# Block sums of the modulation vectors on VectorE in the feed-forward, and later sums with four rows a recurrence step in the first mixer

## The chip, the cores and the metric

The kernel runs on one core of one Trainium2 chip. The metric is the device time of one execution in microseconds (us). The engines are TensorE (PE, whose weight loads are shown apart as PEld), VectorE (DVE), ScalarE (ACT), GpSimd (POOL) and SyncE (SP), whose queue issues most of the DMAs.

## What is computed

The reference is a trunk of two decoder layers over 256 tokens of width 2048, in fp32. Cut to what matters here:

```
cond = silu(c)
for l in range(2):
    mod = (cond @ w_ada[l] + b_ada[l]).reshape(6, 2048)
    sh_m, sc_m, gt_m, sh_f, sc_f, gt_f = mod
    u = x * (1 + sc_m) + sh_m
    proj = u @ w_in[l]
    y_attn = sliding_window_attention(proj ...)      # 16 heads
    y_rwkv = rwkv7_group(proj ...)                   # 16 heads, a recurrence over the tokens
    x = layer_norm(a * x + gt_m * (concat(y_attn, y_rwkv) @ w_out[l]))
    u = x * (1 + sc_f) + sh_f
    x = layer_norm(a * x + gt_f * ((silu(u @ w_gate) * (u @ w_up)) @ w_down[l]))
```

The change concerns the first line of the loop alone: a vector of 2048 numbers times a matrix of 2048 x 12288, for each layer. That matrix is 96 MB a layer and is read once; its product is small, but each of the six pieces is needed at its own point of the layer, so the kernel spreads the work over the run.

## The kernel before

**The weight stream.** All big products go through one scheme. A raw fp32 weight tile comes in by DMA (128 x 1024, four buffers), ACT rounds it to a high part (line 435, three buffers), DVE subtracts to get the low part (line 436, two buffers), and PE makes three matmuls for each piece (lines 457, 458, 460: high by high, high by low, low by high). One such step in the feed-forward is twelve matmuls of 512 columns. PE is to run from step to step without a hole.

**The modulation vectors.** They are made beside that stream in units: a unit is one of the six pieces of one layer, half of it, 1024 columns. For a unit, a generator (`ada_steps`, lines 255 to 281) takes sixteen row steps. Each row step loads 128 rows of the unit (one DMA of 512 KB into the tile `ast`) and makes one DVE operation that adds row times its number of `cond`, per partition, onto the accumulator `aacc` (128 x 1024; line 268 for the first row, line 270 for the rest). Then come `LAG` = 2 empty steps, and then the sum over the 128 partitions. `ada_sums` (lines 316 to 341) does it thus: PE transposes the eight blocks of 128 x 128 (line 327, two PSUM banks of four), ACT copies each with an accumulating output, which adds up its columns (line 331), DVE adds the bias into `mods` (line 334). For a gate (pieces 2 and 5) PE transposes the result (line 339) and a DMA puts it aside as a row.

Two units of the first layer ((0,3,0) and (0,4,1): layer, piece, half) take another way, `ada_direct`: four PE matmuls a row onto four quarters of a bank (`gv`, line 290), with `cond` as the weights.

**What drives the row steps.** In the weight stream `pump` advances the generator by a pace a step (0.75 in the feed-forward of layer 0). In the recurrence of the mixers it is advanced by `adv(AR[l])` at each of the four steps of a recurrence, and in attention by `adv(AA[l])`. The units run in a fixed list, `ada_rest`: in the first mixer (0,2,0), (0,2,1), (0,4,0), then the two direct ones and (0,3,1), then eleven from (0,5,0) on beside the feed-forward of layer 0, and three in the second mixer. `done` holds the finished units; four are finished before the first mixer begins. `side` is set while a feed-forward runs (line 1266, cleared at 1342); then the row tiles take turns between two pools.

**What sets the order.** Within a mixer a string, `ORDER[l]`, gives the order of its operations, which is the order in which the code emits instructions. The final order on each engine is that of a scheduler which simulates when each instruction could run. So an instruction that is emitted elsewhere, or costs something else, can move others.

**Around it.** In the recurrence (lines 837 to 889) PE makes `mr` (lines 841 and 848) for a pair of heads, and then for each of four steps `ob` (lines 868, 871) and the new state `db` (lines 878, 882), which ACT copies. Line 775 is another small product of the same stage, and line 963 a set of transposes for attention. Before the feed-forward and before the next mixer, the residual and the layer norm run on DVE (lines 1335 to 1338, 1132 to 1146), and PE transposes the normalised rows (line 409). There, and only there, the kernel issues matmuls with no use but to keep PE busy: `warm` (lines 104 to 107), eleven before the feed-forward of layer 0 and eight before the second mixer. They write a PSUM bank of the ring from which the sums take theirs.

Of the kernel before, what the change touches and what calls it, by code (L numbers as in the profile page):

```python
# [10 lines left out]
F32 = mybir.dt.float32  # L11
# [3 lines left out]
ALU = mybir.AluOpType  # L15
# [4 lines left out]
P = 128  # L20
# [25 lines left out]
LAG = 2  # L46
WB = (4, 3, 2)
RED = 1
AR = (3, 7)
AA = (1, 45)  # L50
AP = (0.65, 0.3)
AO = (1.1, 2.9)
# [17 lines left out]
def hybrid_trunk_kernel(  # L70
# [21 lines left out]
    def bank(name="mb", tag="mb"):  # L92

        if tag == "cb":
            return ps.tile([P, 512], F32, tag="cb", name=name)
        t = f"m{turn[0]}"
        turn[0] ^= turn[1]
        return ps.tile([P, 512], F32, tag=t, name=name, bufs=1)
# [64 lines left out]
    def prm(l, nm, i, n=1):  # L163
        o = PC[nm] + i
        return par[l][:, o // P, o % P:o % P + n]
# [90 lines left out]
    def ada_steps(l, mod, c0):  # L256

        src = w_ada[l].rearrange("(j p) n -> p j n", p=P)
        n0 = mod * D + c0
        if direct[0]:  # L260
            yield from ada_direct(l, mod, c0, src[:, :, n0:n0 + 1024])
            return
        acc = adap.tile([P, 1024], F32, tag="aacc", name="aacc")
        for j in range(KT):
            t = (side[j % 2:] or [adap])[0].tile([P, 1024], F32, tag="ast", name="ast", bufs=2)
            fetch(t, src[:, j, n0:n0 + 1024], j < 2 and not done)
            if j == 0:
                V.tensor_scalar_mul(acc, t, cond[:, 0:1])
            else:
                ins = V.scalar_tensor_tensor(acc, t, cond[:, j:j + 1], acc, ALU.mult, ALU.add)  # L270
                if anchor:
                    tc.add_manual_dep(ins.ins, anchor[0], order, reason="behind the weight stream")
            yield
        for _ in range(LAG):
            yield

        ada_sums(l, mod, c0, [acc[:, i * P:(i + 1) * P] for i in range(8)])
        done.add((l, mod, c0 // 1024))
        yield

    def ada_direct(l, mod, c0, src):
# [31 lines left out]
        done.add((l, mod, c0 // 1024))  # L313
        yield

    def ada_sums(l, mod, c0, blocks, idle=0):

        col = mod * KT + c0 // P
# [15 lines left out]
        V.scalar_tensor_tensor(mods[l][:, col:col + n], sm[:, 0:n], 1.0 if mod in (1, 4) else 0.0,  # L334
                               prm(l, "b_ada", col, n), ALU.add, ALU.add)
        if mod in (2, 5):
            row = adap.tile([8, P], F32, tag="arow", name="arow", bufs=2)[0:n]
            rb = bank()
            PE.transpose(rb[0:n, 0:P], mods[l][:, col:col + n], ident)
            S.copy(row, rb[0:n, 0:P])  # L340
            dma(gates[l, mod // 3, c0 // P:c0 // P + n], row)

    lead = []

# [1082 lines left out]
```

## Time and profile before

| | |
|---|---|
| median of three runs | 2636.09 us (2634.07 to 2643.67) |
| the profiled execution | 2648.1 us, its span 2646.4 us, mean granted PE clock 0.975 |
| PE busy | 2504.7 us, 95% of the span |
| DVE busy | 1805.9 us, 68% |
| ACT busy | 1185.7 us, 45% |

The profile is that of one execution. A line of it names the engine, the line of the code, the operation, output<-input, and "xN" for N records; an fp32 matmul that is no transpose shows as two records. "[6.26 <-DVE aacc L270]" says that the engine stood idle 6.26 us before this instruction, until DVE had finished the tile aacc on line 270. The granted clock is a share of the full rate.

### The profile page before, as it was taken

To read this page: it belongs to the slowest core of one execution; us is meant where nothing else is said; L and a number is where in the kernel's file an instruction comes from. 1 tells how busy PE (TensorE), PEld (TensorE's weight loads), DVE (VectorE), ACT (ScalarE), POOL (GpSimd) and SP (SyncE) were. 2 spreads that over 40 slices of the span, in tenths; PEclk is the share of its full clock that TensorE was granted. 3 is DMA by queue.
4 is the path that set the end of the run, shared out by engine and by line. 5 is a ranking of instruction groups with operands and counts; after the bars stand their busy time and mean duration, and the time that the engine had idled before them with its cause. 6 is when DMAs were issued, how large, how long until landed. Compare 5 with 4: busy or idle time off the path is not lost.

```text
span 2646.4 us, 42219 instructions
## 1 busy us (share of the span) xinstructions
PE 2504.7 (95%) x15619; PEld 2084.7 (79%) x15619; DVE 1805.9 (68%) x2439; ACT 1185.7 (45%) x2023; POOL 144.7 (5%) x368
## 2 busy tenths in 40 slices
PE   3798998999999999999999999989899999999997
PEld 3797785677888888888888887867788888888887
DVE  7977766579877777777787776565855455545456
ACT  2464453435544444444444544544444443344442
POOL 1003222000000000000000023120000000000000
PEclk9898998999999999999999999989999999999999
DMA  9987657698998888888878685425656655566554
GB/s 371 343 256 238 192 184 248 213 342 289 360 336 304 305 305 312 307 293 308 300 242 301 198 274 163 126 55 202 217 192 189 193 186 194 193 191 191 190 188 147
DMA packets 336384, 637.50 MB, mean 241 GB/s; under 512 B 59511, under 2 KB 126515, under 8 KB 334643
## 3 DMA queue, kind: packets, MB, share of 16 engines
q1 hardware_dynamic: 333170, 629.05, 70.9%
q0 software_dynamic: 1280, 2.62, 0.4%
q10 hardware_dynamic: 1728, 3.15, 0.3%
q8 instruction: 122, 2.00, 0.3%
q14 instruction: 84, 0.68, 0.1%
HBM read 622.08 MB, written 12.62 MB: 240 GB/s over the span
## 4 chain that ended last, share of the span: by engine, by line
PE 79%; DMA 10%; DVE 5%; issue 2%; POOL 2%; ACT 1%; SPq 0%; DVEq 0%; POOLq 0%; ACTq 0%
PE acc L458 20%; PE acc L457 20%; PE acc L460 20%; DMA ast<-in_w_ada_dram 5%; PE acc L471 3%; PE acc L470 3%; PE acc L469 3%; DVE lo L436 1%; DMA raw<-in_w_out_dram 1%; POOL tmp L790 1%; POOL ttl L792 1%; PE mb L1296 1%; DVE aacc L270 1%; PE gv L290 1%; DVE aacc L358 1%
## 5 line engine op out<-in xcount | busy, mean ns | idle before, releaser
L436 DVE TENSOR_TENSOR lo<-raw,hi 128x1024 fp32r<-128x1024 f32 (+2 forms) x728 | 882.0, 1212 | 561.3 <-PE acc L458 375.6
L435 ACT CAST hi<-raw 128x1024 fp32r<-128x1024 f32 (+2 forms) x728 | 758.1, 1044 | 1042.7 <-PE acc L460 836.3
L458 PE MATMUL acc<-lo,u 128*128 128x512 f32 x1568 | 512.8, 394 | 7.8 <-DVE lo L436 7.8
L460 PE MATMUL acc<-hi,u 128*128 128x512 f32 x1568 | 505.7, 391 | 0.0
L457 PE MATMUL acc<-hi,u 128*128 128x512 f32 x1568 | 458.8, 394 | 2.0 <-ACT sg L1289 1.2
L270 DVE SCALAR_TENSOR_TENSOR aacc<-ast,cond,aacc 128x1024 f32<-128x1024 f32 x270 | 345.3, 1279 | 38.9 <-DMA ast<-in_w_ada_dram 38.2
L458 PEld LDWEIGHTS acc<-lo,u 128*128 128x128 f32 x1568 | 294.4, 189 | 71.0 <-DVE lo L436 10.4
L457 PEld LDWEIGHTS acc<-hi,u 128*128 128x128 f32 x1568 | 295.2, 189 | 64.9 <-ACT sg L1289 1.6
L460 PEld LDWEIGHTS acc<-hi,u 128*128 128x128 f32 x1568 | 295.2, 188 | 61.5 <-issue 0.2
L458 PE MATMUL acc<-lo,ht 128*128 128x512 f32 (+1 forms) x720 | 243.3, 377 | 1.5 <-DVE lo L436 1.5
L460 PE MATMUL acc<-hi,ht 128*128 128x512 f32 (+1 forms) x720 | 242.2, 375 | 0.0
L457 PE MATMUL acc<-hi,ht 128*128 128x512 f32 (+1 forms) x720 | 217.0, 376 | 0.0
L469 PE MATMUL acc<-u,hi 128*128 128x256 f32 x720 | 202.9, 289 | 1.9 <-ACT hi L435 1.8
L470 PE MATMUL acc<-u,hi 128*128 128x256 f32 x720 | 202.2, 288 | 0.0
L471 PE MATMUL acc<-u,lo 128*128 128x256 f32 x720 | 190.6, 291 | 5.2 <-DVE lo L436 5.0
L458 PEld LDWEIGHTS acc<-lo,ht 128*128 128x128 f32 x720 | 135.1, 188 | 26.9 <-DVE lo L436 3.1
L460 PEld LDWEIGHTS acc<-hi,ht 128*128 128x128 f32 x720 | 135.6, 188 | 24.3
L457 PEld LDWEIGHTS acc<-hi,ht 128*128 128x128 f32 x720 | 134.8, 188 | 24.3
L469 PEld LDWEIGHTS acc<-u,hi 128*128 128x128 f32 x720 | 141.0, 196 | 5.9 <-ACT hi L435 2.5
L470 PEld LDWEIGHTS acc<-u,hi 128*128 128x128 f32 x720 | 141.0, 196 | 2.8 <-issue 1.7
L471 PEld LDWEIGHTS acc<-u,lo 128*128 128x128 f32 x720 | 132.3, 196 | 9.8 <-DVE lo L436 6.7
L1135 POOL TENSOR_TENSOR brs<-brs,mhalf 128x1 f32<-128x1 f32 x8 | 6.3, 786 | 1685.9 <-DVE brs L1134 765.1
(358 smaller groups left out, 2916.3 us busy)
## 6 DMA issues: line engine op xcount, KB each, us to landing
ast<-in_w_ada_dram SPq DMA_DIRECT2D x368, 512.0 KB
raw<-in_w_gate_up_dram SPq DMA_DIRECT2D x704, 256.0 KB
raw<-in_w_down_dram SPq DMA_DIRECT2D x176, 512.0 KB
raw<-in_w_in_dram SPq DMA_DIRECT2D x82, 512.0 KB
raw<-in_w_out_dram SPq DMA_DIRECT2D x64, 512.0 KB
raw<-in_w_in_dram SPq DMA_DIRECT2D x120, 256.0 KB
ast<-in_w_ada_dram SPq DMA_DIRECT2D x32, 256.0 KB
lnw<-in_ln_w_dram SPq DMA_DIRECT2D x4, 1024.0 KB
```

The source lines that it names most:

```text
L270: ins = V.scalar_tensor_tensor(acc, t, cond[:, j:j + 1], acc, ALU.mult, ALU.add)
L290: PE.matmul(gv[32 * q:32 * q + 32, 0:T], lhsT=cond[:, j:j + 1].to_broadcast([P, 32]), rhs=t[:, q * T:(q + 1) * T], start=(j == 0), stop=(j ...
L358: V.scalar_tensor_tensor(acc, t[:, j], cond[:, j0 + j:j0 + j + 1], acc, ALU.mult, ALU.add)
L435: S.copy(h, fl)
L436: ins = V.tensor_tensor(r, fl, h.bitcast(F32), ALU.subtract)
L457: PE.matmul(bt, lhsT=xh, rhs=hi[:, c0:c0 + w], start=st, stop=False)
L458: PE.matmul(bt, lhsT=xh, rhs=lo[:, c0:c0 + w], start=False, stop=False)
L460: PE.matmul(banks[t][q][:, 0:w], lhsT=xl, rhs=hi[:, c0:c0 + w], start=False, stop=sp_)
L469: PE.matmul(bt, lhsT=hi[:, c0:c0 + w], rhs=xh, start=st and opens, stop=False)
L470: PE.matmul(bt, lhsT=hi[:, c0:c0 + w], rhs=xl, start=False, stop=False)
L471: PE.matmul(bt, lhsT=lo[:, c0:c0 + w], rhs=xh, start=False, stop=sp_ and closes)
L790: G.tensor_tensor(tmp[:, 0:cm, 0:w], nb[:, s:s + 1, s + 1:].to_broadcast([P, cm, w]), tt[:, 0:cm, s:s + 1].to_broadcast([P, cm, w]), ALU.mult)
```

## The change

There are three edits.

1. `AR` goes from (3, 7) to (4, 7): at each recurrence step of the first mixer four rows are asked for, where it was three.
2. The empty steps between the last row of a unit and its sums are six (`3 * LAG`), where they were two, for the units that are reached with at most eight units done and outside a feed-forward: (0,2,0), (0,2,1) and (0,4,0). Inside a feed-forward and later they stay two.
3. Inside a feed-forward the sums over the partitions are made by a new function, `block_sums`. DVE transposes each 32 x 32 block of a half of the accumulator (128 x 512) in one operation, so that the 32 partitions of a block lie along the free axis, and reduces them to 16 numbers; so each of the four groups of 32 partitions has its own partial sum. Four PE matmuls with `fold`, four identity matrices of 32 x 32 stacked over the partitions, add the four groups and put each quarter of the columns on its own 32 output partitions. `fold` is made anew for each unit by three small DVE additions.

```diff
@@ -46,7 +46,7 @@
 LAG = 2
 WB = (4, 3, 2)
 RED = 1
-AR = (3, 7)
+AR = (4, 7)
 AA = (1, 45)
 AP = (0.65, 0.3)
 AO = (1.1, 2.9)
@@ -271,10 +271,13 @@
                 if anchor:
                     tc.add_manual_dep(ins.ins, anchor[0], order, reason="behind the weight stream")
             yield
-        for _ in range(LAG):
+        for _ in range(LAG if side or len(done) > 8 else 3 * LAG):
             yield
 
-        ada_sums(l, mod, c0, [acc[:, i * P:(i + 1) * P] for i in range(8)])
+        if side:
+            block_sums(l, mod, c0, acc, side[1])
+        else:
+            ada_sums(l, mod, c0, [acc[:, i * P:(i + 1) * P] for i in range(8)])
         done.add((l, mod, c0 // 1024))
         yield
 
@@ -313,6 +316,34 @@
         done.add((l, mod, c0 // 1024))
         yield
 
+    def block_sums(l, mod, c0, acc, fp):
+
+        col = mod * KT + c0 // P
+        fold = fp.tile([P, 32], F32, tag="fold", name="fold", bufs=1)
+        V.tensor_add(fold, ident[:, 0:32], ident[:, 32:64])
+        for g in (64, 96):
+            V.tensor_add(fold, fold, ident[:, g:g + 32])
+        part = fp.tile([P, 32], F32, tag="apart", name="apart", bufs=1)
+        for q in range(2):
+            tr = fp.tile([P, 512], F32, tag="atr", name="atr", bufs=1)
+            V.transpose(tr, acc[:, q * 512:(q + 1) * 512])
+            V.reduce_sum(part[:, q * 16:(q + 1) * 16], tr.rearrange("p (b r) -> p b r", r=32), axis=AX.X)
+        b = bank()
+        for q in range(4):
+            PE.matmul(b[32 * q:32 * q + 32, 0:8], lhsT=fold, rhs=part[:, q::4], start=True, stop=True)
+        V.scalar_tensor_tensor(mods[l][:, col:col + 8], b[:, 0:8], 1.0 if mod in (1, 4) else 0.0, prm(l, "b_ada", col, 8), ALU.add, ALU.add)
+        if mod in (2, 5):
+            gate_sums(l, mod, c0, 8)
+
+    def gate_sums(l, mod, c0, n):
+
+        col = mod * KT + c0 // P
+        row = adap.tile([8, P], F32, tag="arow", name="arow", bufs=2)[0:n]
+        rb = bank()
+        PE.transpose(rb[0:n, 0:P], mods[l][:, col:col + n], ident)
+        S.copy(row, rb[0:n, 0:P])
+        dma(gates[l, mod // 3, c0 // P:c0 // P + n], row)
+
     def ada_sums(l, mod, c0, blocks, idle=0):
 
         col = mod * KT + c0 // P
@@ -334,11 +365,7 @@
         V.scalar_tensor_tensor(mods[l][:, col:col + n], sm[:, 0:n], 1.0 if mod in (1, 4) else 0.0,
                                prm(l, "b_ada", col, n), ALU.add, ALU.add)
         if mod in (2, 5):
-            row = adap.tile([8, P], F32, tag="arow", name="arow", bufs=2)[0:n]
-            rb = bank()
-            PE.transpose(rb[0:n, 0:P], mods[l][:, col:col + n], ident)
-            S.copy(row, rb[0:n, 0:P])
-            dma(gates[l, mod // 3, c0 // P:c0 // P + n], row)
+            gate_sums(l, mod, c0, n)
 
     lead = []
 
```

After line 315 the lines of the new kernel have other numbers: 327 is now 358, 409 is 436, 436 is 463, 457, 458 and 460 are 484, 485 and 487; in the recurrence 841, 848, 868, 871, 878, 882 and 290 are 868, 875, 895, 898, 905, 909 and 293.

**In the recurrence of the first mixer.** On PE, the place where the sums of (0,4,0) stand (`mb<-ident,aacc`), between the parts of `mr` of the third group of heads and its first recurrence steps; `gv` are the row sums of the next, direct unit. Before:

```order
L848 MATMUL mr<-am,ah 64x64 x2
L327 MATMUL mb<-ident,aacc 128x128 x4
L848 MATMUL mr<-am,ah 64x64 x3
L775 MATMUL bnb<-xr,bones 128x256
L848 MATMUL mr<-am,ah 64x64
L841 MATMUL mr<-bkt,ah 128x128 x2
L848 MATMUL mr<-am,ah 64x64 x6
L290 MATMUL gv<-ast,cond 32x256 x6
L327 MATMUL mb<-ident,aacc 128x128 x4
L290 MATMUL gv<-ast,cond 32x256 x2
L871 MATMUL ob<-uv,am 64x64 x4
L878 MATMUL db<-uv,bkt 64x64 x4
```

After:

```order
L875 MATMUL mr<-am,ah 64x64 x6
L358 MATMUL mb<-ident,aacc 128x128 x3
L802 MATMUL bnb<-xr,bones 128x256
L358 MATMUL mb<-ident,aacc 128x128
L868 MATMUL mr<-bkt,ah 128x128 x2
L875 MATMUL mr<-am,ah 64x64 x6
L898 MATMUL ob<-uv,am 64x64 x4
L358 MATMUL mb<-ident,aacc 128x128 x4
L905 MATMUL db<-uv,bkt 64x64 x4
L293 MATMUL gv<-ast,cond 32x256 x8
L895 MATMUL ob<-state_1664,rh 64x128 x2
L898 MATMUL ob<-uv,am 64x64 x4
```

The first transposes move from behind two of the `mr` matmuls to behind six, the second four from ahead of `ob` to behind it, and the row sums `gv` from ahead of `ob` and `db` to behind them.

The rest of that recurrence on PE: `state` is the state that ACT copied from the step before. Before:

```order
L963 MATMUL acc<-ident,qr 128x128 x6
L868 MATMUL ob<-state_1664,rh 64x128 x2
L871 MATMUL ob<-uv,am 64x64 x4
L878 MATMUL db<-uv,bkt 64x64 x2
L882 MATMUL db<-state_1664,mt 64x64 x2
L878 MATMUL db<-uv,bkt 64x64 x2
L882 MATMUL db<-state_1664,mt 64x64 x2
L868 MATMUL ob<-state_1665,rh 64x128 x2
L871 MATMUL ob<-uv,am 64x64 x4
```

After:

```order
L905 MATMUL db<-uv,bkt 64x64 x2
L909 MATMUL db<-state_1664,mt 64x64 x2
L293 MATMUL gv<-ast,cond 32x256 x4
L895 MATMUL ob<-state_1665,rh 64x128 x2
L898 MATMUL ob<-uv,am 64x64 x4
L905 MATMUL db<-uv,bkt 64x64 x2
L909 MATMUL db<-state_1665,mt 64x64 x2
L905 MATMUL db<-uv,bkt 64x64 x2
L909 MATMUL db<-state_1665,mt 64x64 x2
L293 MATMUL gv<-ast,cond 32x256 x4
L895 MATMUL ob<-state_1664,rh 64x128 x2
```

Between the recurrence steps stand `gv` rows, one at each step, where before none stood there until the recurrence was over.

**In the feed-forward.** On DVE, the end of one unit and the beginning of the next, in the feed-forward of layer 0: `lo<-raw,hi` is the low part of a weight tile. Before:

```order
L436 TENSOR_TENSOR lo<-raw,hi 128x1024
L270 SCALAR_TENSOR_TENSOR aacc<-ast,cond,aacc 128x1024
L436 TENSOR_TENSOR lo<-raw,hi 128x1024 x3
L268 TENSOR_SCALAR aacc<-ast,cond 128x1024
L334 SCALAR_TENSOR_TENSOR mods_128<-asum,par_124 128x8
L436 TENSOR_TENSOR lo<-raw,hi 128x1024
```

After:

```order
L463 TENSOR_TENSOR lo<-raw,hi 128x1024
L270 SCALAR_TENSOR_TENSOR aacc<-ast,cond,aacc 128x1024
L329 STREAM_TRANSPOSE atr<-aacc 128x512
L463 TENSOR_TENSOR lo<-raw,hi 128x1024
L330 TENSOR_REDUCE apart<-atr 128x16
L329 STREAM_TRANSPOSE atr<-aacc 128x512
L463 TENSOR_TENSOR lo<-raw,hi 128x1024
L330 TENSOR_REDUCE apart<-atr 128x16
L268 TENSOR_SCALAR aacc<-ast,cond 128x1024
L463 TENSOR_TENSOR lo<-raw,hi 128x1024 x2
L334 SCALAR_TENSOR_TENSOR mods_128<-mb,par_124 128x8
```

The two block transposes and the two reductions stand between the low parts of three weight tiles. On PE the four matmuls of this unit (`mb<-apart,fold`) stand ahead of the first matmul that reads the low part made next after line 268; so it is in ten of the eleven units, or with a longer distance, and in the last they stand among the last matmuls of `w_down`.

**Keep-warm matmuls of the second mixer.** On PE, `mb<-rmask,ident`, before the transposes of the normalised rows (`mb<-ident,z`). Before:

```order
L458 MATMUL acc<-wl,ht 128x256
L460 MATMUL acc<-wl,ht 128x256
L107 MATMUL mb<-rmask,ident 128x256 x8
L409 MATMUL mb<-ident,z 128x128 x8
L469 MATMUL lb<-u,hi 128x256
```

After, the same place, and then one of the two places in the stream of `w_down` to which four each have gone:

```order
L484 MATMUL acc<-wl,ht 128x256
L485 MATMUL acc<-wl,ht 128x256
L487 MATMUL acc<-wl,ht 128x256
L436 MATMUL mb<-ident,z 128x128 x8
L496 MATMUL lb<-u,hi 128x256
```

```order
L487 MATMUL acc<-hi,ht 128x512 x2
L484 MATMUL acc<-hi,ht 128x512 x4
L107 MATMUL mb<-rmask,ident 128x256 x4
L485 MATMUL acc<-lo,ht 128x512 x2
L487 MATMUL acc<-hi,ht 128x512 x2
L485 MATMUL acc<-lo,ht 128x512 x2
```

All eight have moved up, some 450 matmuls ahead. Of the eleven before the feed-forward of layer 0, two have moved up among the last matmuls of the output projection in the same way, and nine stand where they stood.

## Prediction

> **What bounds the kernel now.** First the page: engine totals and the chain that ended last.
>
> ```profile
> span 2646.4 us, 42219 instructions
> PE 2504.7 (95%) x15619; PEld 2084.7 (79%) x15619; DVE 1805.9 (68%) x2439; ACT 1185.7 (45%) x2023; POOL 144.7 (5%) x368
> PE 79%; DMA 10%; DVE 5%; issue 2%; POOL 2%; ACT 1%; SPq 0%; DVEq 0%; POOLq 0%; ACTq 0%
> ```
>
> TensorE (PE) is busy 95% of the span. An average hides the stages, so next the windows (columns: length, then busy time of PE, PEld, DVE, ACT and POOL, granted PE clock, DMA share, GB/s).
>
> ```profile
> 400.00:500.00 100.00, 87.63 (x993) 57.50 (x992) 65.19 (x199) 40.79 (x141) 15.94 (x38) 0.88 0.74 233
> 700.00:800.00 100.00, 100.00 (x459) 82.74 (x458) 72.68 (x69) 46.78 (x76) 0.00 (x0) 1.00 0.89 320
> ```
>
> From 700 us on, the feed-forward of layer 0, PE has no hole at full clock (the windows up to 1300 read alike): a microsecond of PE work taken out there is a microsecond of the run, one put in costs as much, and DVE has about 27% of idle time. The recurrence, 400 to 500, is a stage of waits at a reduced clock. PE's waits there and in the output projection behind it:
>
> ```profile
> PE mb L327 <- DVE aacc L270: 6.3, 1, 6.3
> PE acc L457 <- ACT hi L435: 4.3, 2, 4.0
> PE mb L409 <- DVE z L1146: 2.5, 2, 1.7
> PE gv L290 <- DMA ast<-in_w_ada_dram: 2.3, 3, 1.2
> PE ob L868 <- ACT state L887: 2.0, 3, 1.1
> ```
>
> Those five are what the second half of the change could win.
>
> **a. Sums in the feed-forward.** Eleven units lose eight 128x128 transposes on PE and get four 32x8 matmuls. The timeline of PE around one unit before:
>
> ```profile
> 723.43 0.60 PE L327 MATMUL mb<-ident,aacc 128*128 128x128 f32 x4
> ...
> 729.85 1.07 PE L457 MATMUL acc<-hi,u 128*128 128x512 f32 x4
> 732.57 1.07 PE L457 MATMUL acc<-hi,u 128*128 128x512 f32 x4
> ```
>
> A weight step of twelve matmuls is 732.57 - 729.85 = 2.72 us. From 723.43 to 729.85 lie two steps and the eight transposes (four in this row, four in one like it that is left out): 6.42 - 5.44 = 0.98 us a unit. The trace has no 32x8 matmul. Its nearest rows, each plain fp32 matmul being two records:
>
> ```profile
> 179.21 0.63 PE L701 MATMUL ssb<-bones,kkn 128*64 128x2 f32 x8
> 179.76 0.38 PE L471 MATMUL acc<-u,lo 128*128 128x256 f32 x1
> 436.30 0.29 PE L878 MATMUL db<-uv,bkt 128*64 128x64 f32 x4
> 436.42 0.29 PE L882 MATMUL db<-state,mt 128*64 128x64 f32 x4
> 453.25 0.64 PE L290 MATMUL gv<-ast,cond 128*32 128x256 f32 x8
> ```
>
> Four narrow matmuls (L701, eight records) take 179.76 - 179.21 = 0.55 us; at L878's pitch (0.12 us for four records) eight take 0.24. The first is nearest in its few columns, the second in being written to separate parts of the output's partitions, as the new four are. I take the middle, 0.40. Saving: (0.98 - 0.40) x 11 = **-6.4 us**. Ends: -8.1 at 0.24, and 0 if four cost what eight transposes did.
>
> The L290 row bears on this: four 256-column matmuls onto four output quarters take at most 0.64 us there, where one keep-warm matmul of 256 columns takes 0.43 (below). So matmuls onto separate quarters overlap in this trace. The Trainium skill ("TensorE: Matmul & The Clock Gate", "Part 3: Packing small matmuls — row/col tiling") says the same and has such starts some 4 ns apart; by it the four would cost hardly more than one, an estimate of 9 us saved in place of 6.4, which the pitch of L878 does not reach.
>
> Eight ACT copies a unit go as well. They are hidden: ACT is busy 47% there.
>
> DVE receives two 128x512 block transposes, two reductions and three tiny additions a unit (lines of groups by form, and of the window 680 to 1320):
>
> ```profile
> L802 DVE STREAM_TRANSPOSE ytr<-tm 128x512 f32<-128x512 f32 x16 | 11.3, 708 | 36.6 <-DMA tm<-tinv 36.5
> L908 DVE TENSOR_REDUCE vr<-sq 128x8 f32<-128x512 f32 x8 | 5.5, 682 | 6.8 <-ACT sq L906 6.8
> L436 DVE TENSOR_TENSOR lo<-raw,hi 128x1024 fp32r<-128x1024 f32 x228 | 278.9, 1224 | 136.8 <-PE acc L458 79.1 <-issue 50.3 <-DMA raw<-in_w_gate_up_dram 4.0
> L270 DVE SCALAR_TENSOR_TENSOR aacc<-ast,cond,aacc 128x1024 f32<-128x1024 f32 x138 | 176.5, 1279 | 0.1
> L268 DVE TENSOR_SCALAR aacc<-ast,cond 128x1024 f32<-128x1024 f32 x9 | 6.8, 753 | 3.5 <-PE mb L327 3.5
> ```
>
> Added: 2 x 0.71 + 2 x 0.68 + about 0.4 = 3.2 us a unit. The cover is in the same place: between units three row steps carry no accumulation, 3 x 1.28 = 3.8 us, and each weight step has 136.8/228 = 0.6 us of idle DVE, mostly waiting for PE, 2.4 us over the four weight steps of that pause (three row steps at 0.75 a weight step). That is 6.2 us of room for 3.2, so the cost is 0. The new PE wait is covered too: in ten of eleven units the four matmuls stand ahead of a matmul whose lo tile DVE makes after the second reduction, and after at least one other operation (L268, 0.75 us). Behind that wait stands the whole weight stream, so if the cover failed it would be paid in full (rival 2).
>
> **b. Keep-warm matmuls moved.** The scheduler moves all eight of the second mixer some 450 rows up into the full stream, and two of the eleven ahead of the feed-forward.
>
> ```profile
> 611.75 4.91 PE L107 MATMUL mb<-rmask,ident 128*128 128x256 f32 x22
> 1371.43 3.62 PE L107 MATMUL mb<-rmask,ident 128*128 128x256 f32 x16
> 1374.88 0.38 PE L409 MATMUL mb<-ident,z 128*128 128x128 f32 x2
> 1375.81 0.87 PE L409 MATMUL mb<-ident,z 128*128 128x128 f32 x6 [0.54 <-DVE z L1146]
> ```
>
> Before, 1371.43 to 1374.88 lay in time that PE had to wait for the normalisation anyway. The next rows of DVE show why that time does not close:
>
> ```profile
> 1371.63 0.69 DVE L1335 TENSOR_TENSOR tp<-acc,gtf 128x512 f32<-128x512 f32 x1 [1.19 <-PE acc L460]
> 1375.21 1.00 DVE L1146 TENSOR_SCALAR z<-z,brs 128x512 f32<-128x512 f32 x2
> ```
>
> DVE begins the second half when PE's stream ends and needs until 1376.2. So eight matmuls in the full stream cost 3.45 us, and two more 2 x 0.43: **+4.3** (0 if they happen to land in a hole).
>
> **c. Behind them** PE idles 3.4 us longer and the clock may stay halved longer; the last unit's block sums also stand before DVE's L1335. **+1** (0 to +3).
>
> **d. The recurrence of the first mixer.** Sums held back six steps now stand behind four more small matmuls. The rows of PE, then the one of DVE that PE waits for, then the windows:
>
> ```profile
> 424.34 1.09 PE L327 MATMUL mb<-ident,aacc 128*128 128x128 f32 x4 [6.26 <-DVE aacc L270]
> 429.51 1.92 PE L290 MATMUL gv<-ast,cond 128*32 128x256 f32 x12
> 431.36 1.12 PE L327 MATMUL mb<-ident,aacc 128*128 128x128 f32 x4
> 432.40 1.00 PE L290 MATMUL gv<-ast,cond 128*32 128x256 f32 x4
> 433.33 0.45 PE L871 MATMUL ob<-uv,am 128*64 128x64 f32 x8
> ...
> 421.51 2.68 DVE L270 SCALAR_TENSOR_TENSOR aacc<-ast,cond,aacc 128x1024 f32<-128x1024 f32 x2 [2.94 <-DMA ast<-in_w_ada_dram]
> 424.00:432.00 8.00, 7.66 (x45) 4.85 (x46) 3.79 (x10) 2.43 (x10) 6.04 (x26) 0.50 0.79 248
> 440.00:448.00 8.00, 8.00 (x39) 3.67 (x36) 3.00 (x6) 1.66 (x5) 2.97 (x3) 0.50 0.49 135
> ```
>
> PE waits 6.26 us for the accumulation, which waits for its row's DMA, and runs at half clock afterwards (0.50). The Trainium skill ("TensorE: Matmul & The Clock Gate", "Part 1: The HAM clock gate") has about 3.4 us of idle time halve the clock and as much work restore it, as this wait does; by it the hole of c, too, would be followed by some 3.4 us at half clock, an estimate of 1.7 us in place of the 1 that I took. The order of rows on DVE and SP up to here is unchanged, so the wait stays but for four small matmuls, some 0.2 us at L878's pitch. What improves: two groups of row sums (L290) no longer stand ahead of the first state, (431.36 - 429.51) + (433.33 - 432.40) = 2.8 us at half clock. Two later groups now stand between recurrence steps and can each wait for a row, up to the 2.94 us of L270. **-3** (-6, if the slow stretch shortens as much again, to +3, if both wait).
>
> **e. Output projection.** PE's waits and the DMA share:
>
> ```profile
> 563.58 1.22 PE L457 MATMUL acc<-hi,yl 128*128 128x512 f32 x2 [4.00 <-ACT hi L435]
> 504.00:512.00 8.00, 8.00 (x78) 5.42 (x78) 0.85 (x2) 1.26 (x4) 0.00 (x0) 1.00 0.15 43
> 545.00:575.00 30.00, 24.61 (x95) 18.77 (x94) 20.36 (x23) 8.40 (x8) 0.00 (x0) 0.89 1.02 401
> ```
>
> The rows run about four ahead, 2 MB; at 401 GB/s that is 5.2 us of a DMA stretch that is full, if they slip into the idle 504 to 512, and as much delay of the weights if they merely move ahead of them. **-2** (-5 to +3).
>
> **f. Normalisation before the feed-forward.** Two or three more accumulations of 1.28 us stand in DVE's chain while PE waits for it (the L409 row of the waits), where part of the chain waits for other engines: **+2** (0 to +4).
>
> **Sum:** -6.4 + 4.3 + 1 - 3 - 2 + 2 = -4.1 us. The profiled run took 2648.1 (span 2646.4), 12 above the median of 2636.1; the terms are differences, so I set them against the median: **2632.0**. With the ends taken as independent (the roots of the sums of squares of their distances are 6.6 down and 9.3 up), the forecast's own range is 2625 to 2641.
>
> **Rivals.** *1, faster:* holding back really ends the 6.26 us wait. Then PE does not cool, and the 7.66 + 8.00 us at half clock take half: -6.3 - 7.8 = -14.1 in place of d, with e at -5: 2636.1 - 4.1 + 3 + 2 - 14.1 - 5 = 2618. For it: this is the largest single wait there. Against: the order leaves the transposes four matmuls further on.
>
> *2, slower:* block sums make DVE late. Room is 6.2 us, need is 4d + 0.4 with d the length of a transpose or reduction. PE begins to wait at d = 1.45; the run passes +0.5% when the overrun is (13.2 + 4.1)/11 = 1.6 us a unit, d = 1.85. At d = 2.0 it is 2.2 x 11 = 24 us, 2656. Against: 0.68 and 0.71 us in the rows. For: neither row ran beside a full weight stream. The Trainium skill's rules ("VectorE: DVE Perf Modes", "Rules for kernel authors") point this way: a 128x128 transpose belongs on TensorE, and a reduction is the slowest operation of this engine.
>
> *3, it does not do what it says:* the four matmuls cost PE as much as eight transposes, being bound by their weights and the switch. Term a is 0: 2638.4. For: L701's narrow matmuls are slow for their size.
>
> **Numbers.** Forecast 0.57, rival 1 0.26, rival 2 0.09, rival 3 0.08. A measurement of this kernel can tell about 0.5%, 13.2 us (2622.9 and 2649.3). Faster: rival 1, with a tail of the forecast against a tail of its own, 0.26. Slower: rival 2 and a tail of the forecast, 0.10. Same 0.64. The range reaches to rival 1 and leaves out rival 2: 2616 to 2645.
>
> **What would show it.** Right: four matmuls of 0.24 to 0.55 us in place of L327 in the feed-forward, PE still at 100% there; the second mixer's keep-warm rows before 1300 us; a 6 us wait of L327 near 424 still. Wrong: that wait gone (rival 1), a wait of these matmuls or of L458 on DVE in the feed-forward (rival 2), or a full microsecond for the four (rival 3).

## The result, and the profile after

| | before | changed |
|---|---|---|
| median | 2636.32 us (2634.07 to 2643.67, 4 runs) | 2655.86 us (2650.85 to 2658.29, 4 runs) |
| ratio | | 1.0058, interval 1.0043 to 1.0074 |
| profiled execution, span | 2646.4 us | 2656.5 us |

The change makes the kernel about half a per cent slower. I forecast 2632 with a range up to 2645. The page of the changed kernel:

```profile
span 2656.5 us, 42092 instructions
PE 2503.1 (94%) x15619; PEld 2079.3 (78%) x15619; DVE 1833.7 (69%) x2516; ACT 1159.9 (44%) x1847; POOL 143.4 (5%) x368
```

PE's busy time fell by 1.6 us and the span grew by 10.1, so PE stood idle 11.7 us longer. The windows of the two stages that were shown of before (columns as there):

```profile
400.00:500.00 100.00, 81.76 (x997) 54.75 (x995) 61.83 (x195) 40.60 (x142) 17.20 (x38) 0.90 0.73 227
700.00:800.00 100.00, 100.00 (x463) 82.26 (x462) 79.25 (x84) 42.09 (x45) 0.00 (x0) 1.00 0.91 324
```

The feed-forward is as forecast: PE full, DVE busier (79.25 in place of 72.68) and not late. From 400 to 500 PE is busy 5.9 us less: its clock is a little higher (0.90, was 0.88), and it waits more. PE's longest waits from 400 to 700:

```profile
PE oc L942 <- DVE sq L938: 8.0, 1, 8.0
PE mb L358 <- DVE aacc L270: 5.9, 1, 5.9
PE mb L436 <- DVE z L1173: 5.4, 2, 3.5
```

The first row (`oc` and `sq` belong to the group norm behind the recurrence) is not in the profile of before; in a second profile of the kernel before it is 2.2 us. The second is the 6.3 us of before and still there. The third, PE waiting for the normalised rows `z`, is twice the 2.5 of before.

**Stage by stage.** Two executions of one kernel differ before the first changed instruction (the kernel before, run again, is 5.2 us earlier at 395 us), so totals of two profiles can't be subtracted. The table takes PE's instructions that both kernels have, the median of (start in one minus start in the other) at both ends of a stage, and the difference of the two: what the stage gained (-) or lost (+). The first column is the kernel before against itself, the noise of the method: up to 0.4 us as far as 1302 us, 1 to 2 us behind it.

| stage (us) | before, again | changed | changed, again | block sums only | first mixer only | forecast |
|---|---|---|---|---|---|---|
| 395 to 466, recurrence | -0.4 | +1.7 | -0.5 | -1.4 | +1.9 | d -3 |
| 466 to 508, attention | +0.2 | +3.8 | +3.8 | -0.2 | +4.0 | none |
| 508 to 566, output projection | -0.1 | -0.4 | -0.4 | +1.3 | -1.9 | e -2 |
| 566 to 636, normalisation | -0.1 | +3.4 | +5.5 | +0.3 | +3.9 | f +2 |
| 690 to 1270, feed-forward | 0.0 | -4.5 | -4.5 | -4.5 | -0.2 | a -6.4 |
| 1270 to 1302, keep-warm | 0.0 | +3.0 | +3.1 | +3.0 | 0.0 | b +4.3 |
| 1302 to 1555 | -1.3 | -3.7 | -5.5 | -2.7 | -5.9 | c +1 |
| 1555 to 1640, second mixer | +1.7 | +9.3 | +8.5 | -2.1 | +0.6 | none |

The first column of the changed kernel is taken against the first profile of the kernel before, the second against its second; the last two columns, against the second, come from the experiments below. The feed-forward row holds eight of the eleven units of term a, and the keep-warm row eight of the ten matmuls of term b. Two stretches are left out: 636 to 690, where all four changed columns gain 0.9 to 1.6 us, and 1640 to the end, with +1.4 for the kernel before against itself and +1.7, -3.2, -0.2 and +3.7 for the others.

From 395 us to the end the changed kernel loses 13.4 and 5.2 us in these two profiles, and 19.5 and 10.7 in the medians. The columns say where a profile gains and loses; how much the kernel loses in all is told by the medians. The profile of the block sums alone, for one, took 2633.12 us, 9 less than the median of that kernel.

### The profile page after: what moved, and what is told of

Read it like the earlier page. It is cut to its first block, busy times and chain, and to the rows that moved or that the text cites. A ratio compares the mean times of both kernels' runs of the same rounds, so it can differ in the third digit from the quotient of the medians.

```text
span 2656.5 us, 42092 instructions
## 1 busy us (share of the span) xinstructions
PE 2503.1 (94%) x15619; PEld 2079.3 (78%) x15619; DVE 1833.7 (69%) x2516; ACT 1159.9 (44%) x1847; POOL 143.4 (5%) x368
## 4 chain that ended last, share of the span: by engine, by line
PE 78%; DMA 11%; DVE 6%; issue 2%; ACT 1%; POOL 1%; SPq 0%; DVEq 0%; ACTq 0%; POOLq 0%
PE acc L485 21%; PE acc L484 20%; PE acc L487 20%; DMA ast<-in_w_ada_dram 6%; PE acc L498 2%; PE acc L496 2%; PE acc L497 2%; DVE lo L463 1%; DMA raw<-in_w_out_dram 1%; DVE aacc L270 1%; DMA raw<-in_w_in_dram 1%; PE mb L1323 1%; DMA tm<-tinv 1%; DMA raw<-in_w_gate_up_dram 1%; DVE aacc L385 1%
```

## The experiments

My theory after the result: the block sums do what they should and give some 4 us on PE, less 3 for the keep-warm matmuls; the loss is the first mixer's, where the recurrence ends earlier and runs into the inverse of the last group of heads (a matrix that POOL works out for each group of heads and that DMAs carry on to DVE). Rivals: the block sums themselves cost (on DVE, or by the order they bring); or the difference is that of two executions; or the wait for the inverse only shows a lateness that would appear elsewhere. Each ratio is to the kernel before in the same batch. One expectation (the run that orders an inverse first) says that the recurrence runs some 7 us sooner: I had read that from the first pair of profiles, in which the kernel before ran at half clock from 440 to 448 us (0.50), and it is corrected under d below.

**The two kernels again.** The kernel before, unchanged:

> The kernel before, unchanged, for a second profile of it. Order theory (the loss sits in instructions that the scheduler put elsewhere in the two recurrences): this profile has, like the first, the second mixer's third recurrence without the delay of 9 us that the changed kernel shows from 1588 to 1620 us, and differs from the first profile by 5 us at most in any stretch. Scatter theory (waits for DMAs differ by that much from execution to execution of one kernel): this profile differs from the first by 8 us or more somewhere in the two recurrences. Time: 2634 to 2640 us, ratio 1.000.

2638.56 us, ratio 0.9992 (0.9981 to 1.0003). The changed kernel, unchanged:

> The changed kernel, unchanged, for a second profile of it on the chip of the other runs here. Order theory: the delay of 9 us in the second mixer stands again at the same instructions, and the time is 2650 to 2658 us, ratio 1.006 to 1.008. Scatter theory: that delay is gone or half as long, and the time lies near 2645 us.

2650.56 us, ratio 1.004 (1.0027 to 1.0054): the loss is there again, by 10.7 us, so it is not that of two executions.

**The block sums alone**, with three rows a step and two empty steps:

```
-AR = (4, 7)
+AR = (3, 7)
-        for _ in range(LAG if side or len(done) > 8 else 3 * LAG):
+        for _ in range(LAG):
```

> Only the block sums in the feed-forward (four rows a step and the six empty steps undone). Order theory: the feed-forward gains 5 us, the keep-warm matmuls moved into the stream lose 3.5, and the second mixer, whose order moves in this kernel too, loses up to 9: 2640 to 2645 us, ratio 1.002 to 1.003. Scatter theory: no loss in the second mixer, 2634 us, ratio 0.999. A third theory, that the block sums make VectorE late (rival 2 of the prediction), has waits of PE for the low parts in the feed-forward and 2645 us or more.

2642.1 us, ratio 1.0005 (0.9994 to 1.0016): no difference that can be told. **The first mixer's two edits alone**, with the old sums everywhere:

```
-        if side:
-            block_sums(l, mod, c0, acc, side[1])
-        else:
+        if True:
             ada_sums(l, mod, c0, [acc[:, i * P:(i + 1) * P] for i in range(8)])
```

> Only the first mixer's part (four rows a step and six empty steps; all sums by PE transposes as before). The second mixer's order is as before in all but two places. Order theory: the recurrence of the first mixer loses 4.5 us, the normalisation before the feed-forward another 2 to 3, the second mixer nothing: 2641 to 2645 us, ratio 1.002 to 1.0035. Scatter theory: 2636 to 2640 us.

2648.72 us, ratio 1.0035 (1.0023 to 1.0048). The loss is that of the first mixer's edits: the median is 8.9 us above the kernel before, where the whole change has 10.7 and the block sums alone 2.3. PE's waits in this run:

```profile
PE oc L940 <- DVE sq L936: 7.8, 1, 7.8
PE mb L356 <- DVE aacc L270: 6.2, 1, 6.2
PE mb L434 <- DVE z L1171: 5.4, 2, 3.5
```

They are the changed kernel's, to 0.3 us. With the block sums alone PE waits 1.7 us for `sq` and 2.5 for `z`; the two profiles of the kernel before have 0 and 2.2 for `sq`, and 2.5 for `z`. In the table this run loses 7.9 us between 395 and 636, and its profile has 5.0 of them left at the end.

**Keep-warm matmuls held back.** They may not be issued before the last matmul of the weight stream that was emitted ahead of them. The edit holds all of them, also six that the kernel has in the second mixer, near 1730 us, beside the two places named above:

```
     def warm(b, n):
...
-            PE.matmul(b[:, 0:T], lhsT=ident, rhs=rmask, start=True, stop=True)
+            ins = PE.matmul(b[:, 0:T], lhsT=ident, rhs=rmask, start=True, stop=True)
+            if last_mm:
+                tc.add_manual_dep(ins.ins, last_mm[0], order, reason="behind the weight stream")
```

First with the block sums alone:

> Block sums only, and the keep-warm matmuls held behind the last matmul of the weight stream by an order set between them. Theory A (block sums gain 4.5 to 5 us in the feed-forward and lose 3 through the keep-warm matmuls moved into the stream): the second mixer is in the order of before, the loss is gone, ratio 0.998 to 0.999, 2633 to 2636 us beside a before of 2638 to 2640. Theory B (keep-warm matmuls are worth nothing where they stood, and their place does not matter): ratio 1.000 to 1.001 as with block sums alone.

2638.96 us, ratio 0.9997 (0.9984 to 1.0011): by the time alone neither view falls. Then with the whole change:

> The changed kernel with the keep-warm matmuls held in the same way. It also shifts the order in the second mixer. Theory A: 3 us come back before the second mixer; if the 9 us delay at its third recurrence hangs on the order that the changed kernel happened to get there, it is gone too: 2638 to 2640 us, ratio 1.000. Theory B: the delay stands in any order that has the first mixer's part and block sums together: 2647 us, ratio 1.003.

2644.57 us, ratio 1.0016 (1.0003 to 1.0028). In both the stage 1270 to 1302 goes from +3.0 to -0.5, so term b is shown. In the second one the 9 us of the second mixer are gone as well (-1.1 there), though the edit doesn't aim at them: the order came out otherwise. The first mixer's loss stays in it, 9.5 us between 395 and 636.

**No rows at the end of the output projection**, in the kernel with the first mixer's edits alone:

```
             apart = SPLIT_O[l] if c0 == 1536 else 0
+            if apart and l == 0:
+                pace[0] = 0.0
```

> The first mixer's part only, and no rows of the modulation taken during the last piece of the first output projection, so that no accumulation stands in VectorE's chain of the normalisation. Theory A (the accumulations there cost the 3 to 5 us by which all profiles with the first mixer's part fall behind between 570 and 620 us): that step is gone in this profile, and the feed-forward begins 3 us or more sooner than in the kernel with the first mixer's part alone. Theory B (the step comes from the keep-warm matmuls or the clock): it stays at 3 us. The rows left out are taken later, and the order of the second layer moves, so the whole time may go either way by 5 us: 2640 to 2650 us.

2704.2 us, ratio 1.0241 (1.0223 to 1.0258). Between 566 and 636 it gains 2.8 us where the kernel without the pause loses 3.9. DVE's chain there, from the first product of the residual (`z<-acc`) to the last normalised half, takes 9.4 us before with two accumulations in it, 12.8 in the changed kernel and in the one with the first mixer's edits alone, with four and one low part of a weight tile, and 8.7 in this run with none: the normalisation's loss is the rows' accumulations. But the rows that were not taken there must be taken later: some 33 us are lost between 1302 and 1640 and 28 behind, in the second mixer, where DVE then waits for them (DVE's waits, 1450 to 1750):

```profile
DVE aacc L270 <- DMA ast<-in_w_ada_dram: 33.8, 24, 3.0
```

**Each of the two edits of the first mixer by itself.** Four rows a step, two empty steps, old sums; then six empty steps, three rows, old sums; then both again with the block sums and the keep-warm matmuls held.

> Of the first mixer's part only the four rows a recurrence step (two empty steps, sums by PE transposes). The order tells that one unit more is then done before the direct way begins, so that one unit takes it and not two (13 groups of row sums on PE, 31 before). Theory A (the first mixer's part loses through the row sums cut into pieces, 3.3 us, and through rows in the normalisation's chain, 3 to 5 us): with half the row sums there is no loss from pieces; 2636 to 2644 us, ratio 0.999 to 1.002. Theory B (any other order of the recurrences than the old one costs some 5 to 10 us): ratio 1.003 or more.

> Only the six empty steps (three rows a recurrence step, sums by PE transposes). Here too one unit takes the direct way. Theory A: the sums come later while the rows do not come sooner, so the wait of PE for the accumulation near 420 us is gone or moved, and the time lies within 5 us of before: ratio 0.998 to 1.002. Theory B: ratio 1.003 or more.

> Four rows a step, two empty steps, block sums in the feed-forward, keep-warm matmuls held behind the stream: a try at a version that beats before. Theory A: the 4.5 us of the block sums and a microsecond or two of row sums stay: ratio 0.996 to 0.999. Theory B: 1.001 or more.

> Three rows a step, six empty steps, block sums, keep-warm matmuls held behind the stream. Theory A: ratio 0.996 to 0.999. Theory B: 1.001 or more.

| | us | ratio |
|---|---|---|
| four rows only | 2704.58 | 1.0238 (1.0212 to 1.0264) |
| six steps only | 2683.43 | 1.0162 (1.014 to 1.0184) |
| four rows, block sums | 2693.57 | 1.0199 (1.0175 to 1.0222) |
| six steps, block sums | 2661.6 | 1.0078 (1.0055 to 1.0101) |

Either edit alone is worse than both together, against what both views expected. PE's row sums, before and with four rows only, show what else has changed:

```profile
L290 PE MATMUL gv<-ast,cond x256: 379/379/637, 429.5 to 521.2; 128*32 128x256 f32 x128
```

```profile
L291 PE MATMUL gv<-ast,cond x128: 379/634/636, 464.2 to 511.2; 128*32 128x256 f32 x128
```

Half of the 256 records are gone: only one unit is made by the direct way, since which unit is reached when that way is open depends on how fast the rows are asked for. So these four runs test another division of the units, not the two edits one by one; they don't tell how the loss divides between them, and what costs them 22 to 65 us was not followed.

**The inverse behind.** DVE's block transpose `ytr<-tm` waits for a group's inverse, which POOL makes and two pairs of DMAs carry, one out and one back. The changed kernel, on DVE the transpose and two of the instructions that stand behind it (`sq` is what PE waits for), and then PE:

```profile
445.87 0.71 DVE L829 STREAM_TRANSPOSE ytr<-tm 128x512 f32<-128x512 f32 x1 [10.59 <-DMA tm<-tinv]
446.50 0.64 DVE L935 TENSOR_REDUCE vr<-sq 128x8 f32<-128x512 f32 x1
...
449.66 0.69 DVE L938 TENSOR_TENSOR sq<-os__4829,vr 128x512 f32<-128x512 f32 x1 [0.83 <-POOL vr L937]
```

```profile
450.41 1.12 PE L942 MATMUL oc<-ident,sq 128*128 128x128 f32 x4 [7.99 <-DVE sq L938]
```

If the order on DVE is the cause, the transpose behind `sq` should free PE. The first attempt hit the wrong group:

```
-                V.transpose(yt.rearrange("p e s -> p (e s)"), tm.rearrange("p e s -> p (e s)"))
+                tr = V.transpose(yt.rearrange("p e s -> p (e s)"), tm.rearrange("p e s -> p (e s)"))
+                if l == 0 and g == 2 and level == 0:
+                    tc.add_manual_dep(tr.ins, last_sq[0], order, reason="behind the group before")
```

> The changed kernel, with one order set: on VectorE the block transposes that wait for the third group's inverse in the first mixer stand behind the last products of the second group (sq), not ahead of them. Theory A: the first mixer's recurrence does run some 7 us sooner with the change, and loses it because VectorE stands waiting for the inverse's DMA with sq behind it (PE waits 5.4 to 8.0 us for sq in three profiles with the change, 0 to 2.2 in three without): the wait for sq goes below 1 us, the stretch 400 to 480 us gains 3 to 5 us against the changed kernel, and the time falls from 2651 to about 2647 us, ratio to before 1.002 to 1.003. Theory B: the inverse is late for PE as well (its next matmuls need it), so the wait only moves to them: no gain, ratio 1.004.

2660.86 us, ratio 1.0077 (1.006 to 1.0094). The transpose that waits at 446 is that of the fourth group (g == 3), so what this run orders is another one, near 358. By its side effects it shows one thing: here the fourth group's transpose came out ahead of `qr` as well, PE waits for `qr`, and only 1.8 us are left for `sq`.

```profile
PE acc L994 <- DVE qr L987: 8.7, 1, 8.7
```

So I repeated it with `g == 3`, in the changed kernel, in the kernel before, and in the two kernels with the keep-warm matmuls held:

> The changed kernel, with the first block transpose of the inverse of the fourth and last group of heads (DVE, ytr<-tm, line 829, layer 0) ordered behind the sq (line 938) of the third group; the run called e5_inverse_behind moved the transpose of the third group, not this one. If the queue of DVE is what takes the gain of the recurrence (the transpose waits for its data with the three instructions that make sq behind it), PE's wait for sq falls from 5.4 to 8.0 us to under 2, no wait of 5 us takes its place before 480 us, and the run is 5 to 8 us shorter than the changed kernel, a ratio of 0.9965 to 1.002 to the kernel before. If the wait only moves, PE waits as long for the products of the transpose or for the next group's tm, and the ratio stays at 1.003 to 1.008.

2653.93 us, ratio 1.0046 (1.0033 to 1.0059): no faster than the changed kernel. The transpose now stands where it should, and hardly waits:

```profile
442.72 0.69 DVE L938 TENSOR_TENSOR sq<-os__4829,vr 128x512 f32<-128x512 f32 x1
444.53 0.71 DVE L829 STREAM_TRANSPOSE ytr<-tm 128x512 f32<-128x512 f32 x1 [1.11 <-DMA tm<-tinv]
```

PE's two longest waits from 400 to 700 in this run:

```profile
PE gv L293 <- DMA ast<-in_w_ada_dram: 8.0, 8, 1.8
PE mb L358 <- DVE aacc L270: 5.9, 1, 5.9
```

No wait for `sq` of 0.5 us or more is left, and PE waits 8.0 us for the rows instead (2.2 in the changed kernel). The same order in the kernel before:

> The kernel before with the same order: the transpose of the last group behind the sq (line 911) of the third. PE waits for sq 0 to 2.2 us there, so if the queue of DVE is the cause in the changed kernel it can win at most about 2 us here: ratio 0.998 to 1.001. If it is faster by 4 us or more, the order of DVE was a loss in both kernels and explains nothing of the difference.

2645.09 us, ratio 1.0016 (1.0005 to 1.0026), if anything slower, with the same exchange (2.3 and 2.8 us for rows in the two profiles without the new order):

```profile
PE gv L290 <- DMA ast<-in_w_ada_dram: 6.9, 6, 3.2
```

> The changed kernel with the keep-warm matmuls held behind the weight stream, as in e7_after_warm_pinned (ratio 1.0016), and the last transpose behind sq. If the queue of DVE takes the gain, the 5.9 us of that run's wait for sq go and the ratio is 0.998 to 1.000; if the wait only moves, 1.0016 as there. The order changes in other places too, so the wait rows decide, not the time alone.

> The block sums alone with the keep-warm matmuls held and the last transpose behind sq. The run called e6_block_sums_warm_pinned was 0.9997 of the kernel before with a wait of 0.9 us for sq, so both views expect 0.998 to 1.001; this tells whether the block sums can be turned into a version faster than the kernel before.

2652.87 us, 1.0043 (1.003 to 1.0055), and 2655.78 us, 1.0054 (1.0039 to 1.0068). Both are slower than the same kernels without the new order (1.0016 and 0.9997), and than either view expected. In the first, PE waits 7.8 us for rows and `sq` is not among its seven longest waits. Matched as in the table, the recurrence does end some 3 us sooner with the new order (by 466 us, in the changed kernel and in the kernel before), but by 566 nothing of it is left: from 395 the changed kernel has then lost 6.5 us (2.9 without the new order), the kernel before has gained 0.4. So the queue of DVE decides which instruction shows the wait, not how long the stretch to 566 takes: my theory that the inverse holds the first mixer falls, and its rival, that the wait only moves, holds. The new order moves rows on PE too, so this says nothing finer. No version was clearly faster than the kernel before; the block sums with the keep-warm matmuls held equal it.

## Why the prediction was wrong, point by point

The step that failed is the pricing of the moved rows in the first mixer: term d took a gain of 3 us where +1.7 and -0.5 came, it had no term for the same rows in attention (+3.8 twice), and f took 2 where +3.4 and +5.5 came. The largest single miss of the two profiles is a term put at nothing, the second mixer (+9.3 and +8.5).

**What bounds it**: right. From 700 to 1300 PE has no hole in either kernel (599.5 of 600 us busy in both), and what is taken out there is won.

**The range**: the root of the upper ends is 10.5, not 9.3, so the forecast's own range ends at 2642.5; 2655.86 lies outside it even so.

**a, right, size too.** The four matmuls of one unit in the changed kernel, and DVE's two new groups from 680 to 1320 (nine units):

```profile
733.12 1.07 PE L484 MATMUL acc<-hi,u 128*128 128x512 f32 x4
734.12 0.25 PE L333 MATMUL mb<-apart,fold 128*32 128x8 f32 x8
734.30 0.73 PE L485 MATMUL acc<-lo,u 128*128 128x512 f32 x2
734.87 0.62 PE L487 MATMUL acc<-hi,u 128*128 128x512 f32 x2
```

```profile
L329 DVE STREAM_TRANSPOSE atr<-aacc 128x512 f32<-128x512 f32 x18 | 12.8, 710 | 0.5
L330 DVE TENSOR_REDUCE apart<-atr 128x16 f32<-128x512 f32 x18 | 12.2, 676 | 0.0
```

From 733.12 to 734.87 lie 1.75 us for six matmuls of 512 columns and the four; the six take half of the 2.72 us step, 1.36, so the four cost 0.39, as taken (0.40). The four matmuls of eight units lie between 690 and 1270 and give 4.5 us in the table, of which 0.2 comes without the block sums too: 0.54 for each unit, where the forecast had 0.58. DVE's two operations are the 0.71 and 0.68 us of the forecast, and PE doesn't wait for them: rivals 2 and 3 fall.

**b, right, size too.** The +3.0 of the stage stands beside the saving of the one unit that lies in it (-0.5, what is left with the matmuls held), so the eight matmuls cost 3.5 us; the forecast had 3.45. The row below holds four of them (eight records):

```profile
1296.79 1.89 PE L107 MATMUL mb<-rmask,ident 128*128 128x256 f32 x8
1298.33 0.81 PE L485 MATMUL acc<-lo,ht 128*128 128x512 f32 x2
1298.98 0.63 PE L487 MATMUL acc<-hi,ht 128*128 128x512 f32 x2
```

The next pair starts 1.54 us later, and the one behind it after 0.65 where a pair in the full stream takes 0.45: 1.74 for four, 0.43 for each.

**c, about right, but hidden.** The stage behind gains in all columns of the table, 1.3 us even for the kernel before against itself. Matched in the same way, 1302 to 1380 takes 0.1 us more than before in the changed kernel (its second profile) and with the block sums alone, and 2.0 less in the same two kernels with the keep-warm matmuls held. So the moved matmuls do seem to cost 1 to 2 us behind them; of the gain that hides it I have not found the cause.

**d failed.** That the wait stays was right: 5.9 us. From the end of that wait on, the kernel before and then the changed one, on PE:

```profile
433.61 0.40 PE L878 MATMUL db<-uv,bkt 128*64 128x64 f32 x8
...
439.60 0.44 PE L868 MATMUL ob<-state,rh 128*64 128x128 f32 x4 [1.13 <-ACT state L887]
```

```profile
420.76 0.87 PE L358 MATMUL mb<-ident,aacc 128*128 128x128 f32 x3 [5.88 <-DVE aacc L270]
...
426.28 0.70 PE L905 MATMUL db<-uv,bkt 128*64 128x64 f32 x8
426.91 1.68 PE L293 MATMUL gv<-ast,cond 128*32 128x256 f32 x16
...
434.30 0.64 PE L293 MATMUL gv<-ast,cond 128*32 128x256 f32 x8 [1.26 <-DMA ast<-in_w_ada_dram]
434.87 0.44 PE L895 MATMUL ob<-state,rh 128*64 128x128 f32 x4
```

The first state (`db`) comes 433.61 - 424.34 = 9.3 us behind the wait before and 426.28 - 420.76 = 5.5 now: 3.8 us sooner, more than the 2.8 that I took. But the last step (`ob`) comes 15.3 behind it before and 14.1 now: 2.6 of the 3.8 are given back on the way. In the second pair it is 14.9 and 14.6. The rows that no longer stand ahead of the first state stand between the steps, and there they cost their own time again, 1.6 us for two and 0.6 for each single one, and one wait of 1.26. I had written that they "stand between recurrence steps and can each wait for a row", and priced only the waiting: moved work was booked as removed work. What was left of the gain, 0.3 to 1.2 us, met an inverse that comes later: from the end of that wait to DVE's transpose of it are 21.2 us before and 25.1 now, 22.5 and 23.0 in the second pair. Its last two DMAs, before and changed, from issue to landing, and the changed kernel's window in which they run:

```profile
DMA to landing us min/median/max: 3.1/3.2/3.3
```

```profile
DMA to landing us min/median/max: 5.5/5.5/5.5
```

```profile
440.00:448.00 8.00, 2.42 (x30) 1.05 (x28) 2.10 (x4) 0.00 (x0) 1.49 (x3) 0.83 0.70 183
```

They take 5.5 us where it was 3.2, and the DMA share there is 0.70 (0.49 before). In the second pair they take 4.3 (changed) and 3.8 (before), with the first mixer's edits alone 6.0. That the fuller DMA makes them late is argued, not shown: with the block sums alone and the keep-warm matmuls held they take 4.8, without a loss in this stage. Over the stage it comes to +1.7 and -0.5, where the kernel before again has -0.4; d was to be -3.

**The row sums are dearer where they now stand**, for which I had no term: +3.8 from 466 to 508 in both profiles, -0.2 with the block sums alone. PE's busy time for rows between 470 and 550, the kernel before again and then the changed one again:

```profile
470.00:550.00 80.00, 11.01 (x128) 1.00 0.72 249
```

```profile
470.00:550.00 80.00, 14.28 (x128) 1.00 0.70 235
```

The same 128 records take 3.3 us more. The timeline of the changed kernel shows the reason; eight records are one row, four matmuls onto four quarters:

```profile
480.13 0.62 PE L293 MATMUL gv<-ast,cond 128*32 128x256 f32 x2
480.68 0.71 PE L1009 MATMUL acc<-qT 64*128 64x128 f32 x4
481.32 0.63 PE L293 MATMUL gv<-ast,cond 128*32 128x256 f32 x6
481.88 0.33 PE L853 MATMUL ta<-atl,tm 64*64 64x64 f32 x4
...
494.05 0.64 PE L293 MATMUL gv<-ast,cond 128*32 128x256 f32 x8
494.62 0.45 PE L905 MATMUL db<-uv,bkt 128*64 128x64 f32 x8
```

A whole row holds PE 0.57 us, but one quarter 0.55 and three quarters 0.56. Between small matmuls the scheduler cuts rows in two, and each piece costs as much as a row. From 470 to 550 the 128 records stand in 14 pieces in the kernel before and in 20 in the changed one, and six pieces more at 0.55 make 3.3 us. I had read from the row of L290 that quarters overlap, and did not turn it round. The Trainium skill ("TensorE: Matmul & The Clock Gate", "Part 3: Packing small matmuls — row/col tiling") gives the span of such a pack as one matmul and some 4 ns for each more; the trace agrees nearly, at 0.55 to 0.57 us for one to four matmuls, some 6 ns for each more.

**e within its ends, its size too large**: -0.4 in both profiles where the -2 was taken. **f was too small**: +3.4 and +5.5 against +2, and the run with the pause shows that the rows make it. The two more accumulations came as forecast; they cost their full time, and a low part of a weight tile stands in the chain as well.

**The second mixer, +9, had no term at all.** I took its order as the old one but for the keep-warm matmuls. The changed kernel there, DVE and then PE (`rh` is what the recurrence's `ob` reads):

```profile
1592.76 0.35 DVE L884 TENSOR_TENSOR rh<-mr,ar 128x192 f32<-128x192 f32 x1
1593.38 1.28 DVE L270 SCALAR_TENSOR_TENSOR aacc<-ast,cond,aacc 128x1024 f32<-128x1024 f32 x1 [0.28 <-DMA ast<-in_w_ada_dram]
1597.31 1.28 DVE L270 SCALAR_TENSOR_TENSOR aacc<-ast,cond,aacc 128x1024 f32<-128x1024 f32 x1 [2.64 <-DMA ast<-in_w_ada_dram]
...
1598.84 0.35 DVE L884 TENSOR_TENSOR rh<-mr,ar 128x192 f32<-128x192 f32 x1
```

```profile
1599.34 0.69 PE L905 MATMUL db<-uv,bkt 128*64 128x64 f32 x8 [2.93 <-DVE rh L884]
...
1623.29 0.70 PE L895 MATMUL ob<-state,rh 128*64 128x128 f32 x4 [3.29 <-ACT state L914]
```

Two accumulations stand between two `rh` on DVE, and the second waits 2.64 us for its row; PE waits 2.93 behind it and 3.29 later. The kernel before has one there:

```profile
1591.33 0.35 DVE L857 TENSOR_TENSOR rh<-mr,ar 128x192 f32<-128x192 f32 x1
1592.81 1.28 DVE L270 SCALAR_TENSOR_TENSOR aacc<-ast,cond,aacc 128x1024 f32<-128x1024 f32 x1 [1.13 <-DMA ast<-in_w_ada_dram]
...
1594.35 0.35 DVE L857 TENSOR_TENSOR rh<-mr,ar 128x192 f32<-128x192 f32 x1
```

Neither part alone has this loss (-2.1 and +0.6), and it goes when the keep-warm matmuls are held; in that run one accumulation stands between the two `rh` again. So it hangs on the order that the parts give together, which was to be seen before the run. No run moved the one accumulation alone, so that it makes all of the 9 us is argued.

**Rivals.** None came true. Rival 1 needed the 6.26 us wait to end; it stayed. That rival 2's figure for d = 2.0, 2656, lies beside the measured 2655.86 is luck: its mechanism isn't there. The slower outcome came by the dearer rows in attention, by f and by the second mixer, for which I had no rival.

**What stays open**: what sets the end of the stretch from 400 to 566 (the rows' DMAs are what PE waits for when nothing else is late, but no run took them away alone); what of the second mixer's loss is left when the order there is held and all else kept; the gain of 3 to 6 us between 1302 and 1555, of which the noise may be 1 to 2; and how the loss divides between four rows and six steps.

## What to carry to other kernels

Work that moves from ahead of a critical instruction to behind it is not removed: price it again at its new place, with the pieces that the scheduler cuts it into. When a wait is blamed on an engine's queue, move the waiting instruction and look for the wait's next name: if the time of the whole stretch stays and the name changes, the queue was not the cause. Where a scheduler sets the order, compare every later stage that carries the same background work, not only the one that was edited.

## What the runs showed of the hardware that I had not expected

A piece of a row sum, one matmul of 128x256 onto 32 output partitions, holds PE 0.55 us and four such hold it 0.57, so cutting the four in two nearly doubles their cost. Of the kernel before, one profiled execution was 5.2 us earlier than another by 395 us, with the same instructions in the same order, and its later stages agree within 0.4 us up to 1302.
